# Queries and keys projected with channels on partitions, and the scan's decay put on the product of states and C

## The chip, the cores and the metric

The kernel runs on one core of one Trainium2 chip. The metric is the device time of one execution in microseconds (us). The engines are TensorE (PE for its matmuls, PEld for its weight loads), VectorE (DVE), ScalarE (ACT), GpSimd (POOL) and SyncE (SP), which issues most of the DMAs; GpSimd's queue issues some too.

## What is computed

One layer over 1024 latent tokens and 256 context tokens of 1024 channels, in float32. After a normalisation and a modulation (h for latent tokens, hc for context) it runs two token mixers side by side, merges them, and ends with a mixture of 64 experts. The change touches the two mixers:

```python
q, k, v, z, xbc, dt_raw, gates = jnp.split(h @ w_in, IN_SPLITS, axis=-1)
q = apply_rope(q.reshape(nb, ns, N_ATTN_HEADS, 2, ATTN_DH), cos, sin)   # u*cos + rot(u)*sin,
k = apply_rope(k.reshape(nb, ns, N_ATTN_HEADS, 2, ATTN_DH), cos, sin)   # rot swaps halves of 32 of the 64 channels
...
s = jnp.einsum('bqhcd,bkhcd->bchqk', q, k) * ATTN_SCALE                 # 8 heads, 2 components c, 64 channels d
...
cb = jnp.einsum('bcign,bcjgn->bcijg', cc, bc)
y_diag = jnp.einsum('bcijg,bcijgr,bcjgr,bcjgrp->bcigrp', cb, decay, dtc, xc)
y_off = jnp.einsum('bcign,cbgrpn,bcigr->bcigrp', cc, h_prev, jnp.exp(acum))
y = (y_diag + y_off)                                                    # one scan forward, one backward
```

Context tokens have keys and values but no queries, and no rotation. In y_off the factor exp(acum) belongs to a head and a position; the sum over the state n doesn't touch it.

## The kernel before, in words

Every engine's program is written out by hand: tasks are Python generators that yield what they wait for, and a planner (`Flow`, with a cost for each instruction and a due time for each tile) picks the next task by priority and planned time. The order that it finds is fixed when the kernel is built. On the chip each engine runs its queue in that order, and semaphores hold it where data are late. Float32 products are taken as three float32r matmuls of split operands (`mm3`: high x high, high x low, low x high), or as a plain float32 matmul where they are small.

**Query/key/value stage** (`norm_and_qkv`). Six blocks of 512 columns of w_in (k, v, q for heads 0 to 3, then for 4 to 7). The normalised tokens lie with channels on partitions in three groups: 0 is the context (256 tokens), 1 and 2 are 512 latent tokens each. `main` goes over tiles of 128 tokens: 24 matmuls into one of 4 PSUM banks (`acc`), 128 tokens on partitions and 512 channels along them. `post_qk` takes a tile: VectorE multiplies with the cosines and sines (ra, rb), GpSimd adds (r), TensorE transposes r in four pieces into a bank of `tr`, ScalarE and VectorE split it into high and low parts (sa, sb), and after every second tile SyncE stores both into `qk` in DRAM, 64 partitions at a time. `qk` holds, for each head and component, 128 rows: the key's 64 high channels over its 64 low ones, and beside them the query's high part twice and its low part twice. The first block starts with three tiles in halves, channels 0 to 511 first (`NH`), since tokens arrive late. `ada_late` runs on VectorE beside the stage.

**Scan stage** (`mixer_t`). A `server` (lowest priority) feeds TensorE with further projections all through the stage. Beside it four groups of heads are scanned: `states` makes the carried states hp of both directions, `unit` builds W (decay times step size times C.B) for one head and 512 positions, and `decays` makes exp(acum) times C in R, for each direction. `products` then adds up, for each block of 128 positions and each of two heads, three matmuls with 64 output rows in a bank of `py` (ring of 2): x times W, and hp times R forward and backward. `evac` adds the skip and the gate. The rings: 6 tiles R, 2 tiles G, 2 tiles W.

**Attention** (`attention_ahead`, `attention`). For each head and component a tile qk (128 x 3328 elements, 13,312 bytes in each row, ring of 3) is loaded by one DMA of GpSimd's queue (`swdma`, L228). When the last scores of a head's first component are done its tile is freed, and the next head's second component is loaded into it; the scores that need that tile stand two steps behind in TensorE's queue. The v tile of the next head follows on the same queue.

Most matmuls have line L149 and most transposes L153, as helpers issue them.

Of the kernel before, what the change touches and what calls it, by code (L numbers as in the profile page):

```python
# [19 lines left out]
P = 128  # L20
# [8 lines left out]
LEAD = 2  # L29
SLACK = 400.0, 0.0, 200.0, 0.0, 800.0, 400.0, 1500.0  # L30
# [19 lines left out]
def host_consts():  # L50
    j = np.arange(P)
    eye = np.eye(P, dtype=np.float32)
    le = (j[:, None] <= j[None, :]).astype(np.float32)
    ge = (j[:, None] >= j[None, :]).astype(np.float32)
    ones = np.ones((P, P), np.float32)
    cst = np.concatenate([eye, le, ge, ones], axis=1)
    row = np.repeat(np.arange(T // 64, dtype=np.float32), 64)
    col = np.tile(np.arange(64, dtype=np.float32), T // 64)
    inv = np.float32(10000.0) ** (-np.arange(0, 32, 2, dtype=np.float32) / np.float32(32))
    inv = inv.astype(np.float32)  # L60
    ang = np.concatenate([row[:, None] * inv, col[:, None] * inv], axis=-1)
    cos, sin = np.cos(ang), np.sin(ang)
    rope = np.concatenate([cos, cos, -sin, sin], axis=-1).astype(np.float32)
# [313 lines left out]
class Layer:  # L377
# [114 lines left out]
    def norm_and_qkv(s):  # L492
# [28 lines left out]
        st = {"wa": [], "x": 0, "w": 0, "normed": 0, "mod": 0, "done": [set(), set(), set()], "cols": 0, "blocks": 0, "ada": False, "q": None, "two": {}}  # L521
# [114 lines left out]

        def weights():
            for n, (kind, j) in enumerate(blocks):
                c0 = {"q": COL_Q, "k": COL_K, "v": COL_V}[kind] + j * 512
                for a in (0, 4):  # L640
# [8 lines left out]
                    yield from s.splits([(hi[:, b:b + 2], lo[:, b:b + 2], raw[:, b:b + 2]) for b in (0, 2)],  # L649
# [12 lines left out]
        def post_qk(ps, kind, j, t):  # L662
            yield [lambda: st["q"] is not None]
            rr, ras, rbs, sas, sbs, rope = (st["q"][n] for n in ("r", "ra", "rb", "sa", "sb", "rope"))
            if t < 2:
                yield [ps, rr, "ACT"]
                r = rr.get()
                F.acopy(r, ps.rearrange("p (h x) -> p h x", x=64))
                acc.put(ps)
            else:  # L670
                yield [ps, rope, ras, rbs, "DVE"]
                cs = rope[:, t - 2, :]
                pv = ps.rearrange("p (h x) -> p h x", x=64)
                ra, rb = ras.get(), rbs.get()
                F.tt(ra, pv, cs[:, None, 0:64].to_broadcast([P, 8, 64]), ALU.mult)
                F.tt(rb[:, :, 0:32], pv[:, :, 32:64], cs[:, None, 64:96].to_broadcast([P, 8, 32]), ALU.mult)
                F.tt(rb[:, :, 32:64], pv[:, :, 0:32], cs[:, None, 96:128].to_broadcast([P, 8, 32]), ALU.mult)
                acc.put(ps)
                yield [ra, rb, rr, "POOL"]
                r = rr.get()  # L680
                F.ptt(r, ra, rb, ALU.add)
                ras.put(ra)
                rbs.put(rb)
            yield [r, tr]
            pt = tr.get()
            for m in range(4):
                F.tp(pt[:, m * P:(m + 1) * P], r[:, 2 * m:2 * m + 2].rearrange("p u x -> p (u x)"), s.ident)
            two = st["two"].setdefault((kind, j, t // 2), [])
            yield [pt, "ACT"] + ([] if two else [sas, sbs])
            if not two:  # L690
                two += [sas.get(), sbs.get(), 0]
            a, b = two[:2]
            (av, bv), pv = (w.rearrange("p (m h c) -> h p m c", m=4, h=2)[t % 2] for w in (a, b)), pt.rearrange("p (m c) -> p m c", m=4)
            F.acopy(av, pv)
            yield [a, "DVE"]
            F.tt(bv, pv, av.bitcast(F32), ALU.subtract)
            tr.put(pt)
            two[2] += 1
            if two[2] == 2:
                o0 = (t // 2 - (kind == "q")) * 2 * P  # L700
                dst = s.qk[j].rearrange("(m u) (v x) c -> v u x m c", u=2, v=2)
                for w, v, o in ((a, 0, 0), (a, 1, 0), (b, 0, T), (b, 1, T)) if kind == "q" else ((a, 0, 2 * T), (b, 1, 2 * T)):
                    for u in range(2):
                        F.dma(dst[v, u][:, :, o + o0:o + o0 + 2 * P], w[64 * u:64 * u + 64].bitcast(F32).rearrange("x (m c) -> x m c", m=4))
                sas.put(a)
                sbs.put(b)
            rr.put(r)

        def main():
            for n, (kind, j) in enumerate(blocks):  # L710
                tiles = list(range(2 if kind == "q" else 0, 10))
                steps = [(t, 0, KC) for t in tiles]
                if n == 0:
                    steps = [(t, a, a + 4) for a in (0, 4) for t in tiles[:NH]] + steps[NH:]
                banks = {}
                for t, k0, k1 in steps:
                    yield [lambda: len(ready) >= 2 * n + k1 // 4]
                    tok = slice(t * P, (t + 1) * P)
                    g = 0 if t < 2 else 1 if t < 6 else 2
                    sl = slice((t - spans[g][0]) * P, (t - spans[g][0] + 1) * P)  # L720
                    hh, hl = s.h[g]
                    yield [lambda: st["done"][g].issuperset(range(k0, k1))] + ([] if k0 else [acc])
                    ps = banks.pop(t) if k0 else acc.get()
                    for k in range(k0, k1):
# [3 lines left out]
                        s.mm3(ps, hh[:, k, sl], hl[:, k, sl], wh[:, k % 4], wl[:, k % 4], k == 0, k == KC - 1)  # L728
                    if k1 < KC:
                        banks[t] = ps  # L730
                    else:
                        F.spawn(1, post_v(ps, j, tok) if kind == "v" else post_qk(ps, kind, j, t))
                ws = ready[2 * n:2 * n + 2]
                his, los = sets[n % 2]
                for hi, lo in ws:
# [14 lines left out]
        st["q"] = q = {"r": s.ring(qp, [P, 8, 64], "r", 2), "ra": s.ring(qp, [P, 8, 64], "ra", 2),  # L750
                       "rb": s.ring(qp, [P, 8, 64], "rb", 2), "sa": s.ring(qp, [P, 1024], "sa", 2, F32R),
                       "sb": s.ring(qp, [P, 1024], "sb", 2, F32R), "rope": qp.tile([P, 8, P], F32, name="rope")}
        F.dma(q["rope"], I["rope"].rearrange("(t p) c -> p t c", p=P))
# [37 lines left out]
    def mixer_t(s):  # L791
# [10 lines left out]
        if True:  # L802
# [14 lines left out]
            Rs = s.ring(sp, [P, 512], "R", 6)  # L817
            Gs = s.ring(sp, [P, 4, P], "G", 2)
            Ws = s.ring(sp, [P, 4, P], "W", 2)
# [172 lines left out]
            def group(g, x0, x1, B, C):  # L992
# [40 lines left out]
                for pair in range(2):  # L1033
                    for half in range(2):
                        yield [pys]
                        py, ready = pys.get(), []
                        for hh in range(2):
                            yield [(Rs, 2), "NOW"]
                            F.spawn(0, unit(g, pair, half, hh, CB, C, ready))
                        F.spawn(1, products(g, pair, half, xn, hp, py, done, ready, yt))  # L1040
# [39 lines left out]
            def unit(g, pair, half, hh, CB, C, ready):  # L1080
# [4 lines left out]
                R = [Rs.get(), Rs.get()]  # L1085
# [15 lines left out]
                k = []  # L1101
                F.spawn(0, decays(R, C[:, t0:t0 + 512], k, F.clk["DVE"] + 100.0))
# [7 lines left out]
                yield [lambda: len(k) == 2]  # L1110
                ready.append((hh, W, *R))

            def products(g, pair, half, xn, hp, py, done, ready, yt):

                yield [lambda: len(done) == 2 and len(ready) == 2]
                yield [hp[0], hp[1], *(F.ready[_n(q)] + 400.0 for v in ready for q in v[1:])]
                for c in range(4):
                    n = 4 * half + c
                    for i, src in enumerate((xn[:, 2 + n], hp[0][:, n], hp[1][:, n])):
                        for v in ready:  # L1120
                            o = 64 * v[0]
                            x = 128 * pair + o
                            F.mm(py[o:o + 64, c * P:(c + 1) * P], src[:, x:x + 64], v[1 + i].rearrange("p c i -> p (c i)")[:, c * P:(c + 1) * P] if i == 0 else v[1 + i][:, c * P:(c + 1) * P], i == 0, i == 2, 134.5)
                for _, W, R0, R1 in ready:
                    Rs.put(R0, R1)
                    Ws.put(W)
                yield from evac(g, pair, half, py, yt)

            def decays(R, C, k, at):
                for q in R:  # L1130
                    yield [q, at, "ACT"]
                    F.act(q, q, AF.Exp)
                    yield [q, "POOL"]
                    F.ptt(q, q, C, ALU.mult)
                    k.append(1)

            def evac(g, pair, half, py, yt):
# [6 lines left out]
                pys.put(py)  # L1144
                yield [lambda: 2 * g + pair in state["z"], zgs, "NOW"]
# [180 lines left out]
    def attention_ahead(s, go):  # L1326
# [1174 lines left out]
```

## Time and profile before

| what | value |
|---|---|
| runs, us | 2770.72, 2765.67, 2773.66 (median 2770.72) |
| profiled execution, us | 2762.38 |
| its span, first to last instruction, us | 2760.1 |
| mean granted TensorE clock | 0.979 |
| PE / PEld busy | 2610.2 us (95%) / 2099.0 us (76%) |
| DVE / ACT / POOL busy | 2012.4 us (73%) / 1341.9 us (49%) / 920.9 us (33%) |
| chain that ended last, by engine | PE 63%, DMA 8%, DVE 8%, issue 3% |

The stages in the span: up to about 392 us normalisation and q, k, v; up to about 1050 us the scan with the other projections; up to about 1510 us attention; then merge, router and experts. A busy PE counts matmuls from start to modelled end, so neighbours overlap and a full PE is not one at its peak. [...]

### The profile page before, as it was taken

The page shows a single profiled execution, that of the slowest core. Times are in us where ns is not written, and L with a number is a line of the kernel's source. Part 1 is how long each engine was busy: PE and PEld are TensorE (multiplying, and loading weights), DVE is VectorE, ACT ScalarE, POOL GpSimd, SP SyncE. Part 2 cuts the span into 40 slices and gives each one's busy share as a digit, 9 for nine tenths or more (in the row PEclk, how much of TensorE's full clock was granted, in tenths as well). Part 3 has the DMA queues.
Part 4 walks back from the last instruction along what each step waited for, and adds up shares of the span by engine and source line. Part 5 has one row for each costly group of instructions (what it writes and reads, how often), then busy time and mean ns, then how long its engine had stood idle before and what let it go on. Part 6 is the DMA issues. An engine that isn't in the chain of part 4 may idle for free.

```text
span 2760.1 us, 41127 instructions
## 1 busy us (share of the span) xinstructions
PE 2610.2 (95%) x14561; PEld 2099.0 (76%) x14561; DVE 2012.4 (73%) x4680; ACT 1341.9 (49%) x2104; POOL 920.9 (33%) x669
## 2 busy tenths in 40 slices
PE   7999999999999998999999999899999999999992
PEld 4888878878787776888888778677787787777771
DVE  6878133777776657888896657877879898888864
ACT  4211113344444446666675432335566666666652
POOL 0111010445354531000000000044667766777761
PEclk9999999999999999999999999999999999999996
DMA  7767253242425345322422872468999999999998
GB/s 275 226 205 220 62 149 102 69 145 77 138 77 149 91 120 186 119 86 87 142 97 75 263 252 107 168 234 288 292 319 315 339 333 311 315 314 307 296 308 251
DMA packets 275409, 545.67 MB, mean 198 GB/s; under 512 B 31562, under 2 KB 166835, under 8 KB 248194
## 3 DMA queue, kind: packets, MB, share of 16 engines
q1 hardware_dynamic: 238178, 432.95, 46.0%
q0 software_dynamic: 35872, 105.88, 14.7%
q10 hardware_dynamic: 1152, 4.19, 0.4%
q8 instruction: 115, 1.88, 0.3%
q14 instruction: 92, 0.75, 0.1%
HBM read 433.78 MB, written 124.73 MB: 202 GB/s over the span
## 4 chain that ended last, share of the span: by engine, by line
PE 63%; DMA 8%; DVE 8%; issue 3%; POOL 2%; ACT 2%; SPq 0%; ACTq 0%; POOLq 0%; DVEq 0%
PE gu L149 18%; PE acc L149 11%; PE dn L149 9%; PE bacc L149 6%; PE sps L149 5%; PE pv L149 4%; PE xt L153 3%; DMA cr<-cumd,crow 2%; PE tr L153 2%; PE aux L149 2%; DVE G L188 2%; DMA qk<-qk 2%; PE py L149 1%; DVE W L181 1%; PE hT L153 1%
## 5 line engine op out<-in xcount | busy, mean ns | idle before, releaser
L149 PE MATMUL acc<-hh,hi 128*128 128x512 f32 (+2 forms) x760 | 304.8, 401 | 1.3 <-DVE ux L188 1.3
L172 DVE TENSOR_TENSOR gl<-raw,gh 128x1024 fp32r<-128x1024 f32 x240 | 288.7, 1218 | 19.7 <-ACT gh L165 19.4
L149 PE MATMUL acc<-hl,hi 128*128 128x512 f32 (+2 forms) x760 | 289.5, 381 | 0.0
L149 PE MATMUL acc<-hh,lo 128*128 128x512 f32 (+1 forms) x736 | 281.0, 382 | 3.0 <-DVE lo L172 3.0
L149 PE MATMUL gu<-gh,xh 128*128 128x512 f32 (+3 forms) x672 | 279.5, 416 | 0.0
L149 PE MATMUL gu<-gh,xl 128*128 128x512 f32 (+3 forms) x672 | 264.6, 394 | 0.0
L149 PE MATMUL gu<-gl,xh 128*128 128x512 f32 (+3 forms) x672 | 264.3, 393 | 0.2 <-DVE gl L172 0.2
L165 ACT CAST gh<-raw 128x1024 fp32r<-128x1024 f32 x240 | 246.0, 1052 | 30.6 <-PE gu L149 21.2
L263 POOL DMA_INDIRECT cr<-cumd,crow x98 | 134.1, 1368 | 319.0 <-DMA wtab<-sc 282.5
L194 DVE TENSOR_SCALAR_CACHE_REDUCE e<-sps 128x512 f32<-128x512 f32 (+1 forms) x384 | 214.4, 597 | 33.9 <-PE sps L149 33.6
L269 POOL DMA_INDIRECT yacc<-y,tk x98 | 189.4, 1933 | 80.8 <-DMA yacc<-y,tk 14.4
L149 PE MATMUL sps<-qk 128*128 128x512 f32 (+1 forms) x768 | 196.1, 387 | 11.2 <-DMA qk<-qk 6.1
L157 ACT ACTIVATE e<-e,st 128x1280 f32<-128x1280 f32 x128 | 174.8, 1366 | 31.8 <-DVE st L203 31.6
L263 POOL DMA_INDIRECT wc<-wtab,tk x98 | 153.8, 1570 | 86.5 <-DVE tk L183 58.3
L149 PE MATMUL acc<-hi,hh 128*128 128x512 f32 x448 | 182.0, 406 | 0.0
L149 PE MATMUL acc<-hi,hl 128*128 128x512 f32 x448 | 176.6, 394 | 0.4 <-DVE hl L172 0.4
L149 PE MATMUL acc<-lo,hh 128*128 128x512 f32 x448 | 176.6, 394 | 0.0
L149 PEld LDWEIGHTS sps<-qk 128*128 128x128 f32 x768 | 141.4, 192 | 43.9 <-DVE e L194 9.8
L149 PEld LDWEIGHTS acc<-hh,hi 128*128 128x128 f32 (+1 forms) x760 | 142.5, 187 | 32.7 <-issue 4.2
L149 PE MATMUL pv<-wr,vv 128*128 128x256 f32 x640 | 164.6, 380 | 0.0
L149 PEld LDWEIGHTS acc<-hh,lo 128*128 128x128 f32 x736 | 138.8, 189 | 32.9 <-DVE lo L172 4.0
L149 PEld LDWEIGHTS acc<-hl,hi 128*128 128x128 f32 (+1 forms) x760 | 142.6, 188 | 27.4 <-issue 0.8
(327 smaller groups left out, 6246.5 us busy)
## 6 DMA issues: line engine op xcount, KB each, us to landing
raw<-in_w_e_gate_dram SPq DMA_DIRECT2D x64, 1024.0 KB, 9.2
raw<-in_w_e_up_dram SPq DMA_DIRECT2D x64, 1024.0 KB, 11.4
draw<-in_w_e_down_dram SPq DMA_DIRECT2D x64, 1024.0 KB, 9.9
qk<-qk POOLq DMA_DIRECT2D x16, 1664.0 KB, 10.4
raw<-in_w_in_dram SPq DMA_DIRECT2D x40, 512.0 KB, 4.7
wada<-in_w_ada_dram SPq DMA_DIRECT2D x32, 512.0 KB, 5.6
R<-acd SPq DMA_DIRECT2D x64, 256.0 KB, 5.4
qk<-sa SPq DMA_DIRECT2D x52, 256.0 KB, 4.1
```

What stands on the lines that cost most here:

```text
L149: s.nc.tensor.matmul(out, l, r, start=start, stop=stop)
L153: s.nc.tensor.transpose(out, in_, ident)
L157: s.nc.scalar.activation(out, in_, fn, **kw)
L165: s.nc.scalar.copy(out, in_)
L172: s.nc.vector.tensor_tensor(out, a, b, op=op)
L181: s.nc.vector.tensor_scalar(out, a, s1, s2, op0=op0)
L188: s.nc.vector.scalar_tensor_tensor(out, a, sc, b, op0=op0, op1=op1)
L194: s.nc.vector.tensor_scalar(out, a, s1, None, op0=op0, op1=op1, accum_out=acc)
L263: s.nc.gpsimd.indirect_dma_start(out=out, out_offset=None, in_=table, in_offset=bass.IndirectOffsetOnAxis(ap=idx, axis=0), **kw)
L269: s.nc.gpsimd.indirect_dma_start(out=table, out_offset=bass.IndirectOffsetOnAxis(ap=idx, axis=0), in_=in_, in_offset=None, compute_op=ALU. ...
```

## The change

Two parts. In the first, q and k are projected with channels on partitions: a unit is one group of tokens, one half r of the block's 512 channels and one half f of the rotary pair, so that 128 channels (4 head components x 32) lie on partitions and up to 512 tokens along them. The weights are put in that order when they are split. Two units (f = 0, 1) make a pair, and the rotation is four multiplications of whole banks with tables of the same layout, a subtraction and an addition; nothing is transposed. The first block's order becomes two units of group 1, the context's four, then the rest. The stores go from 128 partitions. In `qk` each block of 4 x 32 rows now belongs to one half f and one of high and low, so a tile is gathered by four DMAs of 32 partitions each.

In the second, exp(acum) multiplies the product of hp and C and not C: `carried` loads acum for two heads side by side (E, 64 partitions a head, from the ring of R), takes the exponential, lets TensorE form hp times C for both heads at once (128 x 128 x 128, one bank of `py` for each direction), multiplies on VectorE, and adds the two directions on GpSimd. `products` keeps x times W alone, with 2000 ns of slack behind W in the plan; `evac` adds the carried part.

```diff
@@ post_qk (core)
+            if g:
+                cos, sin = (rope[:, i, (g - 1) * 512:g * 512] for i in range(2))
+                F.tt(l[0], pair[0], cos, ALU.mult)
+                F.tt(rb[:, 1], pair[0], sin, ALU.mult)
+                acc.put(pair[0])
+                F.tt(rb[:, 0], pair[1], sin, ALU.mult)
+                F.tt(l[1], pair[1], cos, ALU.mult)
+                acc.put(pair[1])
+                F.ptt(l[0], l[0], rb[:, 0], ALU.subtract)
+                F.ptt(l[1], l[1], rb[:, 1], ALU.add)
...
+            for f in range(2):
+                for w, v, o in ((hi, 0, 0), (hi, 1, 0), (lo, 0, T), (lo, 1, T)) if kind == "q" else ((hi, 0, 2 * T), (lo, 1, 2 * T)):
+                    F.dma(dst[r, v, f][:, o + o0:o + o0 + n], (w[:, f * 512:f * 512 + n].bitcast(F32) if w is hi else l[f]))
@@ main
+                    units = [(g, r, f) for g in ((0, 1, 2) if kind == "k" else (1, 2)) for r in range(2) for f in range(2)]
+                    if n == 0:
+                        units = units[4:6] + units[:4] + units[6:]
...
+                            s.mm3(ps[:, :spans[g][1] * P], a, b, hh[:, k], hl[:, k], k == 0, k == KC - 1)
@@ products, carried, evac
+                yield [pys, xn, *(F.ready[_n(W)] + 2000.0 for _, W in ready)]
+                        F.mm(py[o:o + 64, c * P:(c + 1) * P], xn[:, 2 + 4 * half + c, 128 * pair + o:128 * pair + o + 64], W[:, c], True, True, 134.5)
...
+                for d in range(2):
+                    for q in range(2):
+                        F.dma(E[d][64 * q:64 * q + 64], bass.AP(tensor=s.acd[d].tensor, offset=s.acd[d].offset + (h + q) * T + t0, ap=[[0, 64], [1, 512]]))
+                for q in E:
+                    F.act(q, q, AF.Exp)
+                for d in range(2):
+                    for c in range(4):
+                        F.mm(py[:, c * P:(c + 1) * P], hp[d][:, 4 * half + c, 128 * pair:128 * pair + 128], C[:, t0 + c * P:t0 + (c + 1) * P], True, True, 218.0)
+                    F.tt(E[d], py, E[d], ALU.mult)
+                F.ptt(E[0], E[0], E[1], ALU.add)
...
+                F.tt(y, y, box[0], ALU.add)
@@ attention_ahead
-                    F.swdma(t, s.qk[h // 4][2 * (h % 4) + c])
+                    for x in range(4):
+                        yield ["POOL"]
+                        F.swdma(t[32 * x:32 * x + 32], s.qk[h // 4].rearrange("(r x) (y i) c -> r y x i c", x=4, y=4)[h % 4 // 2, h % 2 * 2 + c, x])
```

## Rows read from the trace of the kernel before

**Rows 1.** Windows: stage; busy us of PE, PEld, DVE, ACT, POOL; clock, DMA, GB/s

```profile
60.00:400.00 340.00, 333.79 (x1552) 271.06 (x1553) 202.57 (x436) 62.28 (x93) 44.62 (x32) 0.99 0.59 173
490.00:1050.00 560.00, 533.76 (x3033) 440.43 (x3032) 390.80 (x934) 248.90 (x356) 250.44 (x211) 0.98 0.37 113
1050.00:1510.00 460.00, 448.16 (x2493) 386.40 (x2492) 389.50 (x1234) 300.55 (x494) 15.15 (x21) 0.99 0.31 107
```

**Rows 2.** Waits of PE, 60 to 400 us: total us, times, longest

```profile
PE tr L153 <- POOL r L176: 5.6, 3, 2.5
```

**Rows 3.** Waits of PE, 490 to 1015 us

```profile
PE py L149 <- DVE W L172: 14.1, 8, 2.6
PE py L149 <- POOL R L176: 7.3, 9, 3.3
```

**Rows 4.** Windows of 4 us around low clock, columns as in rows 1

```profile
391.00:395.00 4.00, 4.00 (x14) 2.28 (x13) 0.69 (x1) 2.10 (x3) 0.00 (x0) 0.57 0.42 87
...
1213.00:1217.00 4.00, 3.38 (x12) 3.00 (x13) 2.18 (x9) 0.22 (x1) 0.00 (x0) 0.61 1.03 416
```

**Rows 5.** Timeline of PE around one tile's transposes: start, duration

```profile
286.74 0.60 PE L153 MATMUL tr<-cst,r 128*128 128x128 f32 x4
...
287.41 0.40 PE L149 MATMUL acc<-lo,hh 128*128 128x512 f32 x1
287.64 0.40 PE L149 MATMUL acc<-hi,hl 128*128 128x512 f32 x1
```

**Rows 6.** Timeline of PE at the start of the first block

```profile
31.94 0.80 PE L149 MATMUL acc<-hi,hh 128*128 128x512 f32 x1
...
47.68 0.48 PE L149 MATMUL acc<-hi,hh 128*128 128x512 f32 x1
...
58.72 0.60 PE L153 MATMUL tr<-cst,x 128*128 128x128 f32 x4
```

**Rows 7.** Timeline of PE: C times B, and one block of products

```profile
513.58 1.05 PE L149 MATMUL aux<-uC,uB 128*128 128x128 f32 x8
514.39 0.48 PE L149 MATMUL acc<-hh,hi 128*128 128x512 f32 x1
...
671.88 0.61 PE L149 MATMUL py<-R,hp 128*64 128x128 f32 x8
...
672.54 0.61 PE L149 MATMUL py<-R,hp 128*64 128x128 f32 x8
```

**Rows 8.** Groups of instructions, 490 to 1050 us: busy us, mean ns; idle before

```profile
L176 POOL TENSOR_TENSOR R<-R,uC 128x512 f32<-128x512 f32 x64 | 91.6, 1447 | 24.5 <-ACT R L157 16.4 <-DVE yt L188 3.5 <-DVE lo L172 1.8
L188 DVE SCALAR_TENSOR_TENSOR G<-R,ac,G 128x128 f32<-128x128 f32 x128 | 77.9, 671 | 8.4 <-POOL G L176 8.4
...
L188 DVE SCALAR_TENSOR_TENSOR yt<-yt,dcol,py 128x512 f32<-128x512 f32 x16 | 11.8, 736 | 7.2 <-PE py L149 7.2
```

**Rows 9.** Tile G, one instruction: duration in ns, min/median/max; first and last start

```profile
L188 DVE SCALAR_TENSOR_TENSOR G<-R,ac,G x128: 337/345/1385, 525.0 to 992.0; 128x128 f32<-128x128 f32 x128
```

**Rows 10.** Waits of PE, 1040 to 1510 us

```profile
PE sps L149 <- DMA qk<-qk: 6.1, 6, 3.3
```

**Rows 11.** Timeline: PE's longest wait for a tile qk, and GpSimd issuing one

```profile
1213.62 2.22 PE L149 MATMUL sps<-qk 128*128 128x512 f32 x6 [3.31 <-DMA qk<-qk]
...
1314.51 0.53 POOL L228 DMA_DIRECT2D qk<-qk  x1 [49.11 <-PE sps L149]
```

**Rows 12.** Chain that ended last: start, us, what; the load of rows 11

```profile
1314.51 7.32 DMA qk<-qk
```

**Rows 13.** Windows: a 64-partition store alone, with the next; loads; attention's start

```profile
393.30:394.70 1.40, 1.40 (x5) 0.74 (x4) 0.00 (x0) 0.27 (x2) 0.00 (x0) 0.50 0.96 178
394.70:396.10 1.40, 1.40 (x8) 0.82 (x7) 0.00 (x0) 0.00 (x0) 0.00 (x0) 1.00 1.01 302
...
1098.00:1102.00 4.00, 4.00 (x26) 3.56 (x25) 3.75 (x11) 2.96 (x6) 0.56 (x1) 1.00 0.91 362
1041.00:1055.00 14.00, 14.00 (x63) 11.41 (x62) 2.08 (x3) 4.13 (x6) 3.32 (x5) 1.00 0.98 370
```

More of the change, by code (lines that the diff above doesn't have):

```diff
@@ L660, in post_v, with post_qk @@
             sas.put(v)
-        def post_qk(ps, kind, j, t):
+        def post_qk(pair, kind, j, g, r):
             yield [lambda: st["q"] is not None]
[L664 to L682, printed above, removed]
-                rbs.put(rb)
[L684 to L707, printed above, removed]
@@ new lines, in post_qk @@
+            src = l if g else [b[:, :n] for b in pair]
+            yield [sas]
+            hi = sas.get()
+            for f in range(2):
+                yield [src[f], "ACT"]
+                F.acopy(hi[:, f * 512:f * 512 + n], src[f])
+            for f in range(2):
+                yield [hi, "DVE"]
+                F.tt(l[f], src[f], hi[:, f * 512:f * 512 + n].bitcast(F32), ALU.subtract)
+            if g == 0:
+                acc.put(*pair)
+            o0 = (spans[g][0] - 2 * (kind == "q")) * P
@@ L709, in main @@
+            dst = s.qk[j].rearrange("(r v f) p c -> r v f p c", v=2, f=2)
+            for f in range(2):
+                for w, v, o in ((hi, 0, 0), (hi, 1, 0), (lo, 0, T), (lo, 1, T)) if kind == "q" else ((hi, 0, 2 * T), (lo, 1, 2 * T)):
+                    F.dma(dst[r, v, f][:, o + o0:o + o0 + n], (w[:, f * 512:f * 512 + n].bitcast(F32) if w is hi else l[f]))
+            sas.put(hi)
+            sbs.put(lo)
         def main():
             for n, (kind, j) in enumerate(blocks):
-                tiles = list(range(2 if kind == "q" else 0, 10))
@@ L712, in main @@
[L712 removed]
+                if kind == "v":
+                    units = [(0 if t < 2 else 1 if t < 6 else 2, t) for t in range(10)]
+                else:
+                    units = [(g, r, f) for g in ((0, 1, 2) if kind == "k" else (1, 2)) for r in range(2) for f in range(2)]
+                    if n == 0:
+                        units = units[4:6] + units[:4] + units[6:]
+                steps = [(u, 0, KC) for u in units]
                 if n == 0:
[L714 removed]
@@ L1078, in states, with unit @@
                 done.append(d)
-            def unit(g, pair, half, hh, CB, C, ready):
+            def unit(g, pair, half, hh, CB, ready, R):
                 r = 2 * pair + hh
@@ L1129, in decays, with products @@
-            def decays(R, C, k, at):
-                for q in R:
-                    yield [q, at, "ACT"]
-                    F.act(q, q, AF.Exp)
[L1133 to L1137, printed above, removed]
+                ready.append((hh, W))
+            def products(g, pair, half, xn, ready, box, yt):
+                yield [lambda: len(ready) == 2]
+                yield [pys, xn, *(F.ready[_n(W)] + 2000.0 for _, W in ready)]
+                py = pys.get()
+                for c in range(4):
+                    for hh, W in ready:
+                        o = 64 * hh
+                        F.mm(py[o:o + 64, c * P:(c + 1) * P], xn[:, 2 + 4 * half + c, 128 * pair + o:128 * pair + o + 64], W[:, c], True, True, 134.5)
+                for _, W in ready:
+                    Ws.put(W)
+                yield from evac(g, pair, half, py, box, yt)
@@ L1138, in evac @@
+            def evac(g, pair, half, py, box, yt):
                 sl = slice(512 * half, 512 * half + 512)
```

102 lines of the change are left out of this document (63 added, 39 removed).

## The prediction

> **What bounds the kernel now.** I read the stage table first: TensorE is busy 333.8 of 340 us in the query/key/value stage, 533.8 of 560 us in the scan stage and 448.2 of 460 us in attention [rows 1]. In each of the three stages that the change touches, a microsecond that TensorE's queue gains or loses is a microsecond of the end; the stages behind them keep their work. Next the waits of TensorE: it waits 5.6 us for the rotary sum on GpSimd before it can transpose [rows 2], and in the scan 14.1 us for W and 7.3 us for the decayed C in R [rows 3]. Last the granted clock: behind waits of TensorE stand spells of 3.4 us at 0.5 (1.2 GHz), seen as 0.57 to 0.61 in windows of 4 us, like the one after the 3.31 us that it waited for a qk tile [rows 4, 11]. Such a spell loses 1.7 us. There are two behind waits of the first stage, six among the scan's units (two in a row at 726), and that one in attention.
>
> **Query/key/value stage.** The projections of q and k swap stationary and moving operand: 24 matmuls on 512 columns for each 128 tokens x 512 channels become 24 for each 128 channels x 512 tokens, the same columns; I cost them at nothing. What goes:
> - The transposes. From the first of four to the second matmul behind them 0.67 us pass, of which one matmul's step is 0.23 [rows 5]: 0.44 us for a tile. 2 x (10 + 8) = 36 tiles: -15.8 us.
> - The waits on GpSimd's sum in front of them: -5.6 us [rows 2], with the two low-clock spells behind them: -3.4 us.
>
> VectorE's work stays (for 512 tokens four multiplies and two subtractions on 512 columns, as many elements as now), GpSimd's too. The stores to qk become 112 instead of 104, over 128 partitions instead of 64; nothing waits for them here. The planner spreads each pair over two PSUM banks for one more unit (24 x 0.23 = 5.5 us); four banks cover that.
>
> What comes: the first units now need tokens 256 to 767 (group 1), not the context. TensorE began the first halves of the context's tiles 0 and 1 at 31.94, and that of group 1's first tile only at 47.68 [rows 6]. The 24 matmuls before that (5.5 us) filled idle time, and have to be made up when TensorE is full. The second halves then want group 1's channels 512 to 1023, which are transposed up to 58.7 us [rows 6], while now the context's second halves fill in: 2 us more. Bounds: 0, if the planner finds other work, to 12. I take +7.5. Sum of the stage: -15.8 - 5.6 - 3.4 + 7.5 = -17.3 us.
>
> **Scan.** A product unit has now 24 matmuls of 64 output rows in pairs; a block of 128 positions (three pairs) takes 0.66 us at full clock [rows 7], 2.64 us for four blocks. After, W keeps its pair (0.22 us a block) and each direction has one full 128 x 128 x 128 product, like C times B, of which four take 0.81 us [rows 7]. A block: 0.22 + 2 x 0.20 = 0.62; 16 units x 4 x 0.04 = -2 us (rounded down).
> The wait for R goes, since TensorE multiplies the plain C: -7.3 us. Late next is W, and the code gives it 2 us of slack; against that VectorE gets three operations of 512 columns more in each unit, 48 at about 0.7 us (like the one on yt, which reads PSUM too [rows 8]), 34 us. It gets relief too: GpSimd loses 64 products of R with C (91.6 us) and gains 16 sums (about 22 us), and the subtraction into G has a median of 345 ns and a mean of 671 [rows 8, 9], its long ones (up to 1385) where GpSimd works beside it: 77.9 us in place of 44, up to 34 us of stretch. I take these two as even and half of W's waits as gone: -7 us (bounds 0 and -14.1). Half of the six low-clock spells go with them: -5 us (0 to -10).
> What comes: the two PSUM banks of py serve three fillings in a unit instead of one, each freed by VectorE. Every time VectorE is behind the plan TensorE now meets it there, without slack. Bounds: 0, and all that W costs now plus as much again (+28). I take 0.5 us a unit, +8. ScalarE has 32 exponentials less, and SyncE 64 loads more of half size; both run beside TensorE (DMA share 0.37 [rows 1]), and if that cover went a late E would show as a wait of VectorE. Sum: -2 - 7.3 - 7 - 5 + 8 = -13.3 us.
>
> **Attention's loads.** This is where the change can lose. A tile of q and k (128 rows of 13,312 bytes, 1.70 MB) is fetched by GpSimd's queue when scores free its buffer, and the next head's second component is wanted at once: TensorE waited six times of seven, 6.1 us in all [rows 10]. One quiet load took 7.32 us from issue to release [rows 12], and TensorE reaches the scores that need it about 7 us after the issue. So whatever the landing loses, TensorE loses, seven times. After, four transfers of 32 partitions replace one. GpSimd issues one load in 0.53 us [rows 11], so the last quarter goes out some 1.6 us after the first, while the data of the others still move.
> Do 32 partitions move as fast? No row has that load. The nearest: loads on 128 partitions run at 362 GB/s [rows 13], 4.7 us for the 1.70 MB; a store from 64 partitions moves at 178 GB/s as long as it is alone, with all DMA engines busy (0.96), and at 302 GB/s once the other half is in flight beside it [rows 13]. At 178 the tile takes 9.6 us, 4.9 more than at 362; at 302 it takes 5.6, 0.9 more; at full speed 0. The four come in the order lower, lower, upper, upper, so the first two can't help each other as the stores of two halves do: I take +3.5 us a load, nearer to the lone store, 7 x 3.5 = +24.5 us (bounds 0 and +34). Each wait is then about 4 us, past the 3.31 that cost a clock spell [rows 4, 11]: six more spells, 6 x 1.7 = +10.2 (0 to +12). At the start of attention two tiles must land before the first pair of scores can be finished (the DMA engines are busy to 0.98 in the 14 us before [rows 13]); two tiles at 3.5 us more, less 1 us of matmuls between: +6 (0 to +9). The small remainder on GpSimd, 48 issues more, lies in an engine that works 15 of 460 us [rows 1]. Sum: +40.7 us.
> [...]
>
> **Sum.** -17.3 - 13.3 + 40.7 = +10.1 us on the profiled execution's 2762.4 us (span 2760.1 and 2.3 around it). That execution lies 8.3 us below the median of the runs, 2770.7; I put the difference on the median: 2781 us, of itself 2766 to 2798.
>
> **Rivals.**
> 1. The quarters land like the whole, as all 16 DMA engines share each of them by rows. For it: a row of 13,312 bytes is the same, and all engines were busy in the lone store too. Against it: that store's 178 GB/s. Attention then costs +2, the sum is -28.6, 2742 us: faster. It decides if a load lands within 0.5 us of now. Chance 0.22.
> 2. Upper and lower quarters overlap as the store's halves do. A load costs 1.4 us more with the issues, seven 9.8; half of the spells, 5; the start 3: +18, and -13 in all, 2758 us. Chance 0.15.
> 3. The py banks turn into the scan's bound: VectorE is late by the 2 us that it is now at W, and TensorE meets it at more than one of three fillings, 1.5 us more for each of 16 units, +24. For it: two banks, VectorE as the slower engine there. Against it: 70 us less on GpSimd. With the forecast's rest +34, 2805 us. Chance 0.13.
> The forecast itself has 0.50.
>
> **Chances.** A measurement of this kernel tells about 0.3% (8.3 us) from no change, 2762.4 to 2779.0. Faster: nearly all of rival 1 (0.21), over half of rival 2 (0.09), a tenth of the forecast (0.05): 0.35. Within: a third of the forecast (0.17) and the rest of rivals 1 to 3 (0.07): 0.24. Slower: 0.41. The range takes rival 1 in and ends just past rival 3: 2742 to 2808.
>
> **What would show it.** No transposes of r, the stage's end some 17 us earlier; waits of TensorE on W and R under 10 us, and new ones on E's operations; between issue of the first quarter and the scores some 11 us instead of 7.3, with DMA near 180 to 200 GB/s at full share, and a clock of 0.5 behind each. If TensorE's waits on qk stay near 6 us, the forecast is wrong by its largest term; if the scan shows more waits than 21 us, by its second.

## The result, and the profile after

The changed kernel takes 2795.72 us (median of four runs, 2792.99 to 2797.41), the kernel before beside it 2768.4: ratio 1.0096 (95% interval 1.0083 to 1.011), by which it is 26.6 us slower. All ratios here compare the runs of a kernel with runs of the kernel before made beside them. The profiled execution of after took 2795.42 us, span 2793.7.

In the page's forty slices (70 us each) two stand out, the 15th and 16th, 978 to 1117 us, where PE falls to 6 tenths and its clock to 8:

```profile
PE   6999999999999966999999999889999999999992
...
PEclk9999999999999988999999999999999999999996
```

The windows by stage answer to [rows 1], with the end of the scan cut out as a stretch of its own (columns as there):

```profile
60.00:380.00 320.00, 320.00 (x1524) 264.75 (x1523) 200.21 (x407) 61.83 (x94) 42.83 (x32) 1.00 0.55 183
490.00:990.00 500.00, 488.89 (x2615) 407.28 (x2613) 360.99 (x909) 213.22 (x298) 157.85 (x146) 0.99 0.42 127
990.00:1065.00 75.00, 36.31 (x138) 25.98 (x139) 19.00 (x42) 14.23 (x23) 10.96 (x16) 0.75 0.73 180
1065.00:1545.00 480.00, 458.24 (x2514) 391.73 (x2513) 394.24 (x1239) 302.16 (x496) 33.73 (x60) 0.98 0.40 97
```

The first stage is full and the scan is fuller than before. Between the scan and attention TensorE works 36.31 of 75 us, at a mean clock of 0.75. Its waits in that stretch (995 to 1066 us) are for the operands of the branch projections, bacc, which multiply the scan's output (bwh and bwl are the high and low part of a weight, bxh and bxl of the normed output yn; both are loaded as braw and then split):

```profile
PE bacc L150 <- ACT bwh L166: 23.0, 2, 20.5
PE bacc L150 <- ACT bxh L166: 14.0, 2, 13.4
```

The chain that ended last says what they stand behind (start, us, what):

```profile
1005.51 0.67 PE aux L154 x4
...
1011.85 5.94 DMA braw<-in_w_branch_ssd_dram
...
1019.19 2.90 DMA braw<-yn
...
1027.87 31.10 DMA braw<-in_w_branch_ssd_dram
...
1059.72 5.49 PE bacc L150 x12
```

First the last group's norm (its transposes, aux, end at 1006) has to go out as yn and come back, 13 us, in which TensorE has no other work. Then one branch weight of 256 KB takes 31.10 us from issue to landing, while three qk tiles are being read (in the kernel before two such loads beside whole tiles took 19.0 us, behind projections). In the same place before, TensorE still had projections. Groups of PE from the norm's last transposes to the first scores (busy us, mean ns; idle before), before at 1022 to 1055:

```profile
L149 PE MATMUL acc<-hh,hi 128*128 128x512 f32 x34 | 13.5, 398 | 0.0
...
L149 PE MATMUL bacc<-bxh,bwh 128*128 128x512 f32 x12 | 4.8, 399 | 0.5 <-ACT bxh L165 0.5
```

and after at 1006.6 to 1065, with no acc at all:

```profile
L150 PE MATMUL bacc<-bxh,bwh 128*128 128x512 f32 x20 | 10.1, 503 | 37.0 <-ACT bwh L166 23.0 <-ACT bxh L166 14.0
```

The waits that the forecast counted answer to [rows 3] and [rows 10]: for py, none on W and 4.8 us in all on VectorE; for qk 4.9 us.

```profile
PE py L150 <- DVE R L173: 3.6, 2, 2.9
PE py L150 <- DVE yt L189: 1.2, 1, 1.2
```

```profile
PE sps L150 <- DMA qk<-qk: 4.9, 2, 4.0
```

**A ledger of lost time.** From every TensorE record and the trace's stretches of granted clock: lost is the idle time plus half of the busy time at 0.5 (from one matmul of 512 columns to the next 0.427 us pass there, 1.2 columns a ns, and 0.231 at 1.00; medians of before). "Behind the norm" is the number of projection matmuls (acc) that TensorE still has after the last group's norm transposes; they are its cover on the way to attention. "First head" runs from the first scores to the second head's, the rest up to the last scores. Each row but its ratio is read from one execution. The three kinds of change (loads, scan, query/key/value) are told in the experiments.

| kernel | norm ends, us | behind the norm | lost up to there | to the first scores | first head | rest of attention | ratio (interval) |
|---|---|---|---|---|---|---|---|
| before | 1022.0 | 101 | 65.5 | 0.7 | 8.9 | 7.8 | 1 |
| after | 1006.6 | 0 | 49.2 | 42.4 | 11.6 | 17.8 | 1.0096 (1.0083, 1.011) |
| e1, before with quarters | 1019.4 | 101 | 62.9 | 0.7 | 23.8 | 23.1 | 1.0145 (1.0125, 1.0165) |
| e2, after with whole tiles | 1008.6 | 0 | 50.2 | 18.2 | 23.1 | 3.1 | 0.9973 (0.9961, 0.9985) |
| e4, scan's part alone | 1027.7 | 0 | 52.5 | 17.7 | 23.7 | 2.8 | 1.0049 (1.0036, 1.0063) |
| e5, before, less projection | 1017.5 | 37 | 60.4 | 15.2 | 21.1 | 4.8 | 1.0045 (1.0029, 1.0061) |
| e6, query/key/value alone | 1007.5 | 101 | 68.5 | 0.7 | 9.1 | 3.5 | 0.9944 (0.9932, 0.9957) |
| e8, e4 with slack 400 | 1014.0 | 101 | 59.2 | 1.0 | 10.0 | 4.0 | 0.9993 (0.9982, 1.0004) |
| e10, e2 with slack 400 | 993.4 | 101 | 54.4 | 0.6 | 9.1 | 3.2 | 0.9926 (0.991, 0.9942) |
| e12, e4 with projections held | 1020.1 | 95 | 67.8 | 1.1 | 10.8 | 6.2 | 1.0002 (0.9986, 1.0017) |
| e13, after with the same | 1001.6 | 95 | 66.2 | 2.3 | 30.4 | 23.5 | 1.0078 (1.0054, 1.0102) |

The expert stage, from its first matmul to the end, is touched by nothing here. It took 1121.1 us in the trace of before, 1135.5 in that of after, 1115.9 to 1118.3 in the three traces of one chip (e9 to e11) and 1127.7 to 1139.5 in the others, and the traced execution of before lies 6.0 us under the median of the runs beside after. So I compare whole kernels by their ratios and stages by the traces. At the first expert matmul the trace of after is 19.1 us behind that of before (1658.2 and 1639.0); what the expert stage adds to that is not explained.

### The profile page after: what moved, and what is told of

It reads as the page before. It is cut to its first block, busy times and chain, and to the rows that moved or that the text cites. A ratio compares the mean times of both kernels' runs of the same rounds, so it can differ in the third digit from the quotient of the medians.

```text
span 2793.7 us, 40686 instructions
## 1 busy us (share of the span) xinstructions
PE 2603.8 (93%) x14257; PEld 2092.4 (75%) x14257; DVE 2005.8 (72%) x4700; ACT 1320.1 (47%) x2070; POOL 851.5 (30%) x669
## 4 chain that ended last, share of the span: by engine, by line
PE 56%; DMA 8%; DVE 5%; issue 2%; ACT 2%; POOL 0%; SPq 0%; ACTq 0%; DVEq 0%; POOLq 0%
PE gu L150 18%; PE dn L150 10%; PE acc L150 6%; PE bacc L150 5%; PE sps L150 4%; PE pv L150 4%; PE xt L154 3%; PE tr L154 2%; DMA cr<-cumd,crow 2%; DMA braw<-in_w_branch_ssd_dram 2%; PE aux L150 1%; DMA xg<-htab,tk 1%; DMA ysg<-braw 1%; DMA qk<-qk 1%; PE hT L154 1%
## 5 line engine op out<-in xcount | busy, mean ns | idle before, releaser
L150 PE MATMUL acc<-hh,hi 128*128 128x512 f32 (+3 forms) x1080 | 426.4, 395 | 1.5 <-DVE uB L189 1.4
L150 PE MATMUL acc<-hl,hi 128*128 128x512 f32 (+3 forms) x1080 | 407.8, 378 | 0.0
L150 PE MATMUL acc<-hh,lo 128*128 128x512 f32 (+1 forms) x1056 | 399.8, 379 | 0.0
L150 PEld LDWEIGHTS acc<-hh,hi 128*128 128x128 f32 (+1 forms) x1080 | 203.0, 188 | 41.9 <-issue 3.6
L150 PEld LDWEIGHTS acc<-hl,hi 128*128 128x128 f32 (+1 forms) x1080 | 203.0, 188 | 36.4
L150 PEld LDWEIGHTS acc<-hh,lo 128*128 128x128 f32 x1056 | 199.4, 189 | 40.0
L264 POOL DMA_INDIRECT cr<-cumd,crow x98 | 128.0, 1306 | 316.3 <-DVE hl L173 279.5
L270 POOL DMA_INDIRECT yacc<-y,tk x98 | 183.8, 1875 | 89.7 <-issue 14.9
L150 PEld LDWEIGHTS sps<-qk 128*128 128x128 f32 x768 | 141.5, 193 | 47.6 <-DVE e L195 13.4
L264 POOL DMA_INDIRECT xg<-htab,tk x98 | 128.0, 1306 | 93.0 <-PE hT L154 53.6
L150 PE MATMUL bacc<-bxh,bwh 128*128 128x512 f32 x256 | 113.0, 441 | 46.2 <-ACT bwh L166 23.0
L166 ACT COPY wr<-tr 128x512 f32<-128x512 f32 x160 | 93.2, 582 | 127.2 <-PE tr L154 127.0
```

The source lines that it names most:

```text
L150: s.nc.tensor.matmul(out, l, r, start=start, stop=stop)
L166: s.nc.scalar.copy(out, in_)
L264: s.nc.gpsimd.indirect_dma_start(out=out, out_offset=None, in_=table, in_offset=bass.IndirectOffsetOnAxis(ap=idx, axis=0), **kw)
L270: s.nc.gpsimd.indirect_dma_start(out=table, out_offset=bass.IndirectOffsetOnAxis(ap=idx, axis=0), in_=in_, in_offset=None, compute_op=ALU. ...
```

## The loads: e1, e2, e3

Theory A: the reading in quarters costs. Theory B: TensorE's projections run out. e1 puts the quarters into the kernel before:

```diff
-                    F.swdma(t, s.qk[h // 4][2 * (h % 4) + c])
+                    for x in range(4):
+                        yield ["POOL"]
+                        F.swdma(t[32 * x:32 * x + 32], s.qk[h // 4][2 * (h % 4) + c][32 * x:32 * x + 32])
```

> The kernel before with one edit: a qk tile is read by four transfers of 32 partitions, all else as it was. Theory A (a transfer into 32 partitions moves at about half the rate, and while the first three tiles are read, whatever else TensorE needs stands behind them): the packets of the qk loads take about 1000 ns instead of 512, a load 8.5 to 10 us instead of 5 to 7, first scores 6 to 9 us later, head changes 1 to 3 us longer each, in all 15 to 25 us slower, 2783 to 2793. Theory B (the loads cost little; the change lost its gain because TensorE's projections are used up before attention can start): within 5 us of the kernel before.

Measured 2805.89 us against 2769.57, ratio 1.0145: by the ratio 40 us slower (36 by the medians), more than either theory gave. The median packet of a tile row took 994 ns instead of 513. With 101 projections behind the norm only 0.7 us are lost before the first scores, but 14.9 us more in the first head and 15.3 in the others. That is 30 of the 40 us; the traced execution (2797.59 us) is 8.3 under the median of its runs, and the rest isn't placed. TensorE's waits (1040 to 1560 us): a branch weight and the tile itself, where it had been 6.1 us for the tile [rows 10].

```profile
PE bacc L149 <- ACT bwh L165: 12.6, 2, 9.3
PE sps L149 <- DMA qk<-qk: 9.5, 3, 4.5
```

e2 takes the quarters out of the changed kernel. The stores interleave the rows in DRAM, so that a tile is 128 neighbouring rows again:

```diff
-            dst = s.qk[j].rearrange("(r v f) p c -> r v f p c", v=2, f=2)
+            dst = s.qk[j].rearrange("t p c -> (t p) c").rearrange("(r p v f) c -> r v f p c", r=2, v=2, f=2)
@@ loads
-                    (the four transfers)
+                    F.swdma(t, s.qk[h // 4][2 * (h % 4) + c])
```

> The changed kernel with the rows of qk in DRAM interleaved by the stores (row = 4 x partition + quarter), so that a tile is again 128 neighbouring rows and is read by one transfer of 128 partitions; queries and keys lie in the same new order. Theory A: packets back near 512 ns, the wait of 31 us for a branch weight at 1028 us gone, some 30 of the 43 us that TensorE lost between 990 and 1065 us and most of the 12.6 us more in attention come back: 2756 to 2768. Theory B: the 13 us idle at 1007 us and most of the rest stay, 2785 to 2796.

Measured 2762.8 us, ratio 0.9973; from 1.0096 that is 34 us. Packets are at 513 ns again. Theory A has its number, yet B is not gone: 13.2 us of idle time before the first operands remain, and 7.3 for a weight behind them (waits of PE, 1008 to 1094 us).

```profile
PE bacc L150 <- ACT bxh L166: 13.2, 1, 13.2
PE bacc L150 <- ACT bwh L166: 7.3, 1, 7.3
```

e3 keeps four transfers of 32 rows and changes only the partitions that each goes to:

```diff
-                        F.swdma(t[32 * x:32 * x + 32], ...
+                        F.swdma(t[x::4], ...
```

> The changed kernel, still four transfers of 32 rows for a tile, but each goes to every fourth partition instead of 32 neighbours (the order of the channels is the same for q and k). If it is the neighbouring partitions that halve the rate: as the whole tile, within 8 us of it, packets near 512 ns. If it is that a transfer has 32 rows only, or that there are four: packets stay near 1000 ns and the time at 2790 to 2800.

Measured 2768.14 us, ratio 0.9997 (0.9987 to 1.0008), within 8 us of the whole tile; packets 512 ns. So neither the number of transfers nor their 32 rows halve the rate, but that the 32 partitions are neighbours. The windows in which the first three tiles land (columns as in [rows 1], the last is GB/s), before, after and e3:

```profile
1043.20:1060.40 17.20, 17.06 (x75) 13.09 (x73) 5.94 (x19) 5.96 (x8) 1.12 (x2) 1.00 1.00 380
```

```profile
1028.30:1055.60 27.30, 7.58 (x29) 4.83 (x27) 2.08 (x3) 1.23 (x2) 4.74 (x9) 0.74 1.10 215
```

```profile
1031.00:1045.90 14.90, 6.74 (x29) 4.82 (x27) 1.87 (x3) 0.62 (x1) 5.28 (x10) 0.82 1.04 396
```

At 215 GB/s the DMA engines are as busy as at 380 or 396 (share 1.10, 1.00, 1.04): they are held twice as long by the same bytes (a packet of a tile row takes 1002, 513 and 512 ns in after, before and e3), and a branch weight of that stretch takes 31.10 us to land in after. The 6.6 us between e3 and e2 are not settled; the planner costs four issues more than one and orders TensorE otherwise (60 branch matmuls before the first scores, 36 in e2).

## The parts alone: e4 and e6

e4 is the kernel before with the scan's part only, e6 with the query/key/value part only (and whole tiles, as in e2); their diffs are those parts of the change.

> The kernel before with the scan's part of the change alone; queries, keys and their loads as before. If what TensorE saves in the scan (17 us less lost time in the trace, 2 to 5 us less work) reaches the end: 2748 to 2756. Theory B: the scan's units end no earlier, since they follow VectorE and the rings, the projections run out sooner, and the gain is idle time ahead of attention: 2763 to 2773. By the forecast's terms: -13 us, 2755.

Measured 2783.58 us, ratio 1.0049: 13.6 us slower, outside both expectations. TensorE's lost time up to the norm did fall, 65.5 to 52.5, but the norm ends 5.7 us later and no projection is left behind it: 17.7 us are lost before the first scores and 23.7 in the first head. The waits of TensorE from the norm on (1027 to 1113 us) are much like those of e2:

```profile
PE bacc L150 <- ACT bxh L166: 13.1, 1, 13.1
PE bacc L150 <- ACT bwh L166: 7.8, 1, 7.8
```

> The kernel before with the query/key/value part of the change alone, and the rows of qk interleaved so that a tile is still read by one transfer of 128 partitions; the scan as before. By the forecast's term -17.3 us: 2752. From the runs so far (whole tile with both parts 2762.8, scan alone 2783.6, before 2769.6): if the parts add up, -20.8 us, 2749. Theory C holds here too, since the scan's chain starts as many microseconds earlier as the stage ends: first scores 16 to 20 us earlier.

Measured 2754.4 us against 2770.82, ratio 0.9944: 15.5 us faster, near the forecast's 17.3. The stage up to 382 us has no idle time (PE 322.00 of 322 us), the norm ends 14.5 us earlier, and the 101 projections still stand behind it.

```profile
60.00:382.00 322.00, 322.00 (x1529) 266.29 (x1529) 199.64 (x406) 62.18 (x94) 42.72 (x32) 1.00 0.56 182
```

## The premise: e5 and e9

If TensorE's queue set the end of the scan's stage, taking work from it had to help. e5 shortens two projections of the kernel before:

```diff
+                            cut = kind == "g" and q >= 14
+                            F.mm(b[:, :n], hi[:, k], hh[:, k], k == 0, cut and k == KC - 1)
+                            if cut:
+                                continue
```

> The kernel before with work left out: the last two of the sixteen gate projections keep only the product of the high parts (64 matmuls of 512 columns fewer, 64 x 0.23 = 14.7 us of TensorE's queue, in the last stretch ahead of attention), so their values are rounded. Premise of the forecast (a microsecond that TensorE's queue loses in the scan's stage is a microsecond of the end): 14.7 us faster, 2755. Theory C (the chain of the scan's groups sets when attention can start, the projections only fill TensorE beside it): 0 to 4 us faster, with new idle time of TensorE between the last projection and the first scores.

Measured 2781.91 us against 2770.82: ratio 1.0045, with 14.7 us of matmuls less it is 12 us slower. Neither expected that. 37 matmuls are left behind the norm instead of 101, and the two waits of the scan's part appear (1017 to 1108 us):

```profile
PE bacc L149 <- ACT bxh L165: 9.8, 2, 9.6
...
PE bacc L149 <- ACT bwh L165: 6.3, 1, 6.3
```

e9 is the reverse, the scan's part alone with 64 matmuls more in the last four gate projections (`if kind == "g" and q >= 12: F.mm(b[:, :n], lo[:, k], hl[:, k], False, False)`):

> The scan's part alone, with work added: the last four gate projections also take the product of the two low parts (64 matmuls of 512 columns more, 64 x 0.23 = 14.7 us of TensorE's queue, ahead of attention). Premise of the forecast (TensorE's queue sets the end of the stage): 14.7 us slower than the scan's part alone (2783.6), 2798. Theory C (projections cover the chain from the scan's last y to the first branch operands and the first head's weights; in the scan's part alone TensorE lost 18.6 us between the last y and the first scores and 23.7 in the first head, 0.7 and 8.9 before): the added work falls into idle time, not slower, and 5 to 15 us faster if the first head's loss goes too, 2768 to 2784.

Measured 2772.3 us where the kernel before took 2754.37: ratio 1.0064 (1.0043 to 1.0084), against 1.0049 without the work; 4 us more, and the intervals overlap. So neither 14.7 us slower nor faster. In the traces, of one execution each and on two chips, the first expert matmul comes 10.8 us after that of e4: most of the added work was paid there. The chain that ended last shows why theory C was too simple:

```profile
1032.87 0.44 PE aux L154 x4
1033.31 2.81 PE acc L150 x12
1036.12 0.44 PE aux L154 x4
1036.56 4.68 PE acc L150 x20
1041.23 0.15 SPq L214
...
1041.43 5.97 DMA braw<-in_w_branch_ssd_dram
```

The planner put most of the added work ahead of the norm's transposes (aux), which end at 1036.6 instead of 1027.7; 19 matmuls stand behind them. What covers the way to attention is how many projections come behind the norm, not how many there are in all.

## Two edits of the scan: e7 and e8

e7 moves the load of the gate tile z in `evac` up to that of y, ahead of the wait for py; e8 sets `F.ready[_n(W)] + 400.0` for 2000.0 in `products`. Both are edits of the scan's part alone.

> The scan's part alone, with one edit: the gate tile z is loaded when the unit's skip tile is, ahead of the wait for the product, and not after the carried part was added. Theory C1 (the end of each group got longer, since the two last units' z loads of 5 us stand behind one more step; VectorE waits 20.7 us for z in seven waits, 6.9 in three before): z waits under 7 us, the scan ends 8 to 14 us earlier, 2770 to 2777 in all. Theory C2 (the order in which the planner puts the longer chain, or the six R tiles that now serve 96 fillings instead of 64): z waits go, others take their place, within 4 us of the scan's part alone (2783.6).

Measured 2766.61 us against 2770.82, ratio 0.9983: 18 us better than e4, more than expected, though the waits on z fell only from 20.7 to 12.4 us. 86 projections are behind the norm.

```profile
DVE yt L173 <- DMA zg<-zs: 12.4, 3, 4.4
```

> The scan's part alone, with the slack behind W in the plan at 400 ns, as before the change, instead of 2000. If the slack only moves waits of TensorE into planned room for projections: waits of py on W come back (up to 14 us as before), the scan's units end within 3 us of where they did, the time 0 to 8 us slower than the scan's part alone. If the slack lengthens the chain (16 units, 1.6 us at the end of each group at least): 6 us or more faster.

Measured 2768.04 us, ratio 0.9993: 15.5 us better than e4, as the second expectation had it. Waits of TensorE on W come back, 10.1 us in 8, so by the row it is worse in the scan (lost 59.2 up to the norm, 52.5 in e4), and in all it is better: 101 projections are behind the norm, which ends 13.7 us earlier.

```profile
PE py L150 <- DVE W L173: 10.1, 8, 2.2
```

Each of two unlike edits restores the cover and brings the norm forward, so neither tells by itself whether the shorter chain or the cover does it.

## Projections held back: e12 and e13

Theory D changes nothing but the order: the last two gate projections wait for the last norm.

```diff
+                    if kind == "g" and q >= 14:
+                        yield [lambda: state["turned"] == 8]
@@ norm, behind the transposes
+                    state["turned"] += 1
```

> The scan's part alone, with the last two gate projections (96 matmuls, 22.5 us) held back until the last group's norm has had its transposes; nothing else changes but the order. In the runs so far 101 matmuls of projections stand behind these transposes in TensorE's queue where the way to attention costs little (0.6 to 1.0 us lost before the first scores, about 9 in the first head), and none where it costs 18 to 19 and 23. Theory D (the scan's part loses because its slack lets the projections be used up before the norm): 96 behind the norm, the two losses fall to about 1 and 10 us, the norm comes a little earlier, 2758 to 2770 on a chip where the kernel before takes 2769.6. Rival (the scan's longer chain, the last y 12 us later, is the loss, and the projections then only move): 2779 to 2787.

Measured 2771.35 us against 2770.43, ratio 1.0002: 13 us better than e4, a microsecond past the range of theory D and outside the rival's. Behind the norm, from 1020.1 to the first scores at 1050.9, TensorE has 32 of each projection matmul and waits for nothing before bacc:

```profile
L150 PE MATMUL acc<-hh,hi 128*128 128x512 f32 x32 | 13.3, 415 | 0.0
...
L150 PE MATMUL bacc<-bxh,bwh 128*128 128x512 f32 x11 | 4.3, 390 | 0.0
```

The losses fall to 1.1 and 10.8 us, while the loss in the scan rises to 67.8, as the waits there are no longer filled. The scan's part then is worth nothing, and costs nothing: up to the first expert matmul TensorE has 7.0 us less to do than before and loses 3.1 us more.

> The changed kernel as it is, its loads in four quarters too, with the same two projections held back behind the last norm. Theory D: the idle time ahead of the first branch operands (13 us) goes; the quarters' loss stays, since the branch weights still stand behind three tiles at half the rate: 10 to 18 us faster than the changed kernel (2795.7), 2778 to 2786, and the rest, 12 to 20 us over the kernel before, is the quarters' share less the gain of the query/key/value stage. If the quarters are hidden once TensorE has projections to work on: 2765 or less.

Measured 2792.78 us, ratio 1.0078; 3 to 5 us under the changed kernel, with overlapping intervals, not 10 to 18. The first scores come at 1037.8 instead of 1065.0, and the first head then takes 67.2 us instead of 46.6, with a branch weight missing again (waits of PE, 1001 to 1105 us):

```profile
PE bacc L150 <- ACT bwh L166: 18.4, 2, 18.1
```

So with quarters in the kernel moving the cover buys almost nothing: 40 us less are lost before the first scores, but 17 more up to the norm and 24 more in attention. That the loads and the missing cover overlap in time, and that the loads set the end here, fits this and is not shown apart.

## A version ahead of both: e10 and e11

e10 is e2 with the slack of e8, e11 has the early z as well.

> The changed kernel with whole tiles and the slack behind W at 400 ns. Theory C: the scan's last y comes some 15 us earlier, projections are left over to cover the way to attention, the losses between the last y and the first scores and in the first head fall from over 30 us to about 11; W's waits return with some 10 us. If the gains of the parts add up (query/key/value -16, scan with this slack -2): 2752 or less. Else near the whole tile alone, 2763.

Measured 2732.36 us where the kernel before took 2754.37: ratio 0.9926 (0.991 to 0.9942), 20 us faster than before, as theory C expected; waits on W are back with 10.5 us. Against e6 that leaves some 5 us for the scan's part, 6 either way. 101 projections are behind the norm, which ends at 993.4; from there to the first scores TensorE works 32.31 of 32.9 us.

```profile
993.40:1026.30 32.90, 32.31 (x138) 25.66 (x138) 10.56 (x21) 14.44 (x22) 4.03 (x5) 1.00 0.78 261
```

> The changed kernel with whole tiles, the slack at 400 ns and z loaded ahead of the wait for the product. If both edits shorten the end of the groups by themselves: a few us under the whole tile with the slack alone, 2742 to 2750. If one is enough, or the planner's order decides: within 4 us of it.

Measured 2741.83 us, ratio 0.9961 (0.9946 to 0.9976): 10 us behind e10, which neither expectation had. Two edits that each help alone don't add up; here 149 projections stand behind the norm, 75.2 us were lost up to it, and the first scores come 18.8 us later than in e10.

## Why the prediction missed

The direction and the range held, the size did not: +10.1 forecast, +26.6 measured. By the ratios nearly all of the excess of 16.5 us lies in one term, the scan's.

- **Query/key/value, -17.3:** measured -15.5 (e6, 11.9 to 18.8 us by its interval). No transposes of r, no wait on GpSimd, no idle time from 60 us to the stage's end. The first units began at 46.80 us, as forecast from [rows 6]; the first 60 us have 38.77 us of PE at clock 0.91 where there were 41.28 at 1.00.
- **Attention's loads, +40.7:** measured 40 in e1 (34.6 to 45.7) and 34 between after and e2. The sum came near by luck, since its parts were wrong. By the prediction's own sign (waits on qk near 6 us) this term fails. A load's last packet lands 9.8 us after the first issue instead of 7.1 (medians of the seven loads at a head's change): +2.7, forecast +3.5. TensorE does not lose that seven times, since its waits on qk are 9.5 us in e1 and 4.9 in after. The forecast had 34.7 us at the heads and 6 at the start; e1 lost 15.3 more at the later heads and 14.9 more in the first. Six more clock spells were forecast; from the second head to the last scores after has two, before one. I counted what the tile itself makes TensorE wait, and left out the branch weights, of which one of 256 KB took 31.10 us beside the tiles and 5.94 ahead of them (after).
- **Scan, -13.3:** this is the term that failed. Alone it measured +13.6 (e4). In the changed kernel it is what is left of 1.0096 over the product of e1 and e6 (1.0145 x 0.9944 = 1.0088): 0.08%, +2 us with some 8 either way. That is 15 of the 16.5 us of excess.

The traces split it another way. At the first expert matmul query/key/value alone is 18.3 us ahead of before (e6), the quarters alone 29.1 behind (e1), the scan alone 7.9 behind (e4): 18.7 together, and after is 19.1 behind. There the loads stand 11.6 us under their forecast and the scan 21.2 over. These are single executions, so sizes are good to several us; ratios and traces agree that the scan's gain never reached the end.

Within the scan the rows came out nearly as worked out: no waits on R as TensorE's operand or on W, 4.8 us on VectorE's operations on E and y where 8 were allowed, though 4.8 us of new waits on GpSimd's G came in (0.2 before); the 48 new operations take 35.0 us (34 forecast), GpSimd's sums 22.2 (22). The stretch of VectorE behind GpSimd shrank, as forecast from [rows 8, 9] (mean of the subtraction in after; 671 ns before):

```profile
L189 DVE SCALAR_TENSOR_TENSOR G<-R,ac,G 128x128 f32<-128x128 f32 x128 | 48.9, 441 | 0.9 <-POOL G L177 0.9
```

In before all 41 subtractions over 500 ns had GpSimd at work during at least 88% of their time, and the 18 without it took 338 to 341 ns; in after 14 are over 500 ns.

TensorE's lost time up to the norm fell by 13.0 us in e4 and 16.3 in after. The step that failed stands ahead of the sum: "In each of the three stages that the change touches, a microsecond that TensorE's queue gains or loses is a microsecond of the end." A share of 533.8 of 560 us [rows 1] showed a full queue, not that the queue set the end. In the scan it was full because projections filled what the chain of groups (states, units, norm) left free, and the chain's end sets when the branches and attention can begin. In after and e4 the plan put every projection ahead of the norm (with 400 ns of slack behind W, e8, or z early, e7, 101 and 86 stay behind it); the first branch operands come some 13 us after the norm's transposes whatever is saved (13.1 us before, 13.4 after, 13.1 in e4), and what had covered them was gone. e5 shows it without the change, and e12 by the order alone: there the same scan costs nothing. Neither gives the 13.3 us back, as projections that cover the way to attention no longer fill the waits of the scan. For the kernel with quarters the share of the cover stays open, since e13 gained only 3 to 5 us.

**The rivals.** That quarters land like the whole is refuted by 994 and 1002 ns a packet instead of 513. That halves overlap partly: the order lower, lower, upper, upper gave 215 GB/s with other traffic in it; another order was not tried. That the py banks bind the scan: waits on py are 4.8 us, so not by that mechanism, though its time (2805) came out nearer than the forecast's.

**The rate of the loads.** From first packet to last, the seven tiles at the heads' changes moved at 154 to 205 GB/s in quarters of 32 neighbouring partitions (after), 199 in the middle, and at 213 to 296 whole (before), 288 in the middle. Over every fourth partition three tiles landed in 14.9 us (e3), over 32 neighbours in 27.3 (after). Why neighbouring partitions are slower, no run shows.

## What to carry to other kernels

A full engine need not set the end of a stage: ask what the queue would hold at the next hand-over if the stage were cheaper, and count the filler that stands behind the last link of the chain. Price a transfer not by who waits for it alone but by how long it holds the DMA engines and what else is wanted in that time. And spread each transfer of a tile over the partitions: four over every fourth partition (e3) cost 27 us less here than four over 32 neighbours (after).

## What was not expected of the hardware

With all 16 DMA engines at a share of 1.0 to 1.1 in each case, three tiles (5.1 MB) landed in 27.3 us (quarters of 32 neighbouring partitions) or in 14.9 (every fourth partition), so the busy share of the engines told nothing of the rate. And a load of SyncE's queue, 256 KB, took 5.94 us ahead of the tiles of GpSimd's queue, 31.10 us beside three of them in quarters, and 19.0 us beside three whole ones (before): a queue of its own gave it no cover here.
